# A hybrid mLSTM and attention layer on one core: the first block's sums and splits in another order, and its first loads on two queues

## The chip, the cores and the metric

The kernel runs on one core of one Trainium2 chip. The metric is the device time of one execution in microseconds (us). The engines are TensorE (PE; its weight loads are PEld), VectorE (DVE), ScalarE (ACT), GpSimd (POOL) and SyncE (SP), whose queue issues nearly all transfers. The profile is of one execution, and Lnn is line nn of the kernel.

## What is computed

One layer of a streaming encoder over 2048 prompt tokens and 8 x 16 sample tokens, width 1024, in float32:

```python
qm, km, vm, om, ip, fp, qa, ka, va = split_in(x @ w_in)
hm, C1, n1, m1 = mlstm_chunkwise(qm, km, vm, logi, logf, C0, n0, m0, mchunk)   # 4 heads of 128
ha = swa_prompt(qa, ka, va, attn_sinks)                                         # or swa_step for the samples
mix = jnp.concatenate([hm, ha], axis=-1) @ w_out
h = layer_norm(DEEPNORM_ALPHA * x + mix, ln1_g, ln1_b)
f, conv_rows = conv_ffn(h, conv_prev, w_up, w_conv, b_conv, w_down)
y = layer_norm(DEEPNORM_ALPHA * h + f, ln2_g, ln2_b)
```

The case touches only the beginning of `x @ w_in`.

## The kernel before

**Splits.** Every operand of a matmul is split into a high part, which ScalarE casts (L218 for weights, L569 for tokens: `oh`), and a low part, which VectorE subtracts (L219; L570: `ol`). A product then takes three matmuls: high by high, high by low, low by high.

**Blocks and products.** The tokens go through the input projection in blocks. Block 0 has the four token tiles 0 to 3, 128 tokens each, and the sample tile 16. For each of five groups `g` of output columns, the product of the block with the weights is formed in Strassen's manner from seven products of half-sized blocks. They are numbered 1 to 7; (b, g, s) is product s of group g in block b. The products need sums of quarters of the tokens (`x_steps`: t3, t2, t4 and t1, each a VectorE pass over 128x1024) and of quarters of the weights (`split_first`, L505 to L522). The tokens' quarters are the loads 1 to 4 (`xr1` to `xr4`; load 3 holds the second half of the columns of tokens 0 and 1, and serves product 2). Ahead of the products stand direct products of each token tile with the gate and key weights `wg` (`i_direct`, L739), in four pieces. The order of products in block 0 is: the direct ones of tokens 0 and 1 (first halves of both, then second halves), of tokens 2 and 3, (0,0,1), the direct one of the sample tile, (0,0,2), (0,1,1), (0,0,7), (0,0,6), (0,0,5), (0,0,4), (0,0,3), (0,1,7). A product's result is gathered in one of three PSUM banks; products 6, 5 and 3 share one, and 7 and 4 another, so each of them waits until ScalarE or VectorE (L779, L783) has read the bank.

**Order.** TensorE's instructions keep the order in which the program is written. The other engines' orders are made by a scheduler from the order in which the program asks for them, with `i_after` (the reading of banks) at high priority. Each engine then runs its own row strictly in turn. `next_raw` asks for a weight's load and `next_split` for its split; `advance` asks for as many of both as there are buffers. A transfer takes one of eight completion semaphores in rotation, and so is issued only when the eighth transfer before it has landed.

`x_load` loads token quarters, `x_steps` sums and splits them, `x_single` does so for the sample tile. Before the change all of block 0's steps are asked for ahead of the loop over products. `warm_up` runs nine matmuls on zeros before any data comes. `t_setup` loads small constants (`k_sink`, `kw` and others), which VectorE prepares at L956 to L966.

Of the kernel before, what the change touches and what calls it, by code (L numbers as in the profile page):

```python
# [205 lines left out]
class Prog:  # L206
# [20 lines left out]
    def run(self):  # L227
        PS = bass.MemoryType.PSUM
        nb = len(OBLOCKS)
        with ExitStack() as es:  # L230
            def enter(*a, **k):
                cm = self.pool(*a, **k)
                return cm.__enter__(), cm
            close = lambda cm: cm.__exit__(None, None, None)
            self.cp = es.enter_context(self.pool("const"))
            self.dp = es.enter_context(self.pool("dram", space=bass.MemoryType.DRAM))
            es.enter_context(self.tc.manual_schedule(engines={mybir.EngineType.PE}))
            self.setup()
            self.wp = es.enter_context(self.pool("wsb"))
            self.dps = es.enter_context(self.pool("dps", 3, PS))  # L240
            self.tp, tcm = enter("tsb", side="right")
            self.tps, tpcm = enter("tps", 5, PS)
            self.xp, xcm = enter("xsb")
            self.mp, mcm = enter("isb")
            chains = Chains(self)
            self.xs, self.gates, self.i_done = {}, {}, 0
            self.i_begin()
            self.warm_up()
            chains.weave(self.i_dense())
            close(mcm)  # L250
            wx, wxcm = enter("wx1sb")
            self.unit_more(wx)
            self.mp, mcm = enter("osb")
            self.o_setup()
            for b in range(nb - 1):
                chains.weave(self.late_done(self.o_block(b)))
            chains.until(NPT - 1)
            chains.drain()
            close(tpcm)
            close(tcm)  # L260
            self.fp, fcm = enter("fsb", side="right")
            self.fup, fpcm = enter("fup", 3, PS)
            self.f_setup()
            dense = self.o_block(nb - 1)
            first = self.f_hT(0)
            next(first)
            n = 0
            for i, _ in enumerate(dense):
                if i >= 2:
                    next(first, None)  # L270

                if i in (4, 7, 10):
                    self.f_tokens(0, *{4: (1,), 7: ("t1",), 10: ("t3", 7, "t2", 6)}[i])

                if i >= 22 and n < (2, 4, 5)[min((i - 22) // 4, 2)]:
                    self.f_next()
                    n += 1
            for _ in first:
                pass
            assert not self.norms  # L280
            close(mcm)
            close(wxcm)
            close(xcm)

            self.wx, wxcm = enter("wx2sb")
            self.f2, f2cm = enter("f2sb")
            self.f3, f3cm = enter("f3sb")
            self.f_ups(n)
            close(f3cm)
            close(f2cm)  # L290
            self.f2, f2cm = enter("d2sb")
            self.f3, f3cm = enter("d3sb")
            self.f_downs()
            for cm in (f3cm, f2cm, wxcm, fpcm, fcm):
                close(cm)
# [238 lines left out]
    def x_load(self, b, *qs):  # L534
        for q in qs:
            self.xr[b, q] = r = self.x_raw(q)
            x = self.a["xq"][b][(q - 1) // 2, (q - 1) % 2]
            n = 2 if (b, q) == (0, 1) else 1
            for i in range(n):
                k = slice(i * 4 // n, (i + 1) * 4 // n)  # L540
                self.nc.sync.dma_start(r[:, k], x[:, k])

    def x_steps(self, b, *steps):

        nc, V = self.nc, self.nc.vector
        r = lambda q: self.xr[b, q]
        for s in steps:
            if s == "t3":
                self.spare = False
                self.xt = e = self.raw_slot([P, 4, HT]) if b else [self.tp.tile([P, 4, HT], F32, name="xt", tag="qk", bufs=2), False]  # L550
                V.tensor_sub(e[0], r(4), r(2))
            elif s == "t2":

                V.tensor_add(self.xt[0], self.xt[0], r(1))
            elif s == "t4":

                V.tensor_sub(r(4), r(3), self.xt[0])
                self.xt[1] = True
            elif s == "t1":

                V.tensor_sub(r(2), r(2), r(1))
            else:
                x = self.xt[0] if s in (7, 6) else r({1: 1, 2: 3, 3: 4, "b12": 2, 5: 2, 4: 4}[s])

                self.hx[b, s] = h, l = self.x_slot(4 if s == "b12" else s)
                n = 4 if (b, s) == (0, 1) else 1
                for i in range(n):
                    k = slice(i * 4 // n, (i + 1) * 4 // n)
                    nc.scalar.copy(h[:, k], x[:, k])  # L569
                    V.tensor_sub(l[:, k], x[:, k], h[:, k].bitcast(F32))  # L570

    def x_single(self, *steps):

        nc, V = self.nc, self.nc.vector
        raw = self.single_raw
        for i in steps:
            src = raw[:, 4:] if i > 1 else raw[:, :4]
            if i == 4:
                V.tensor_sub(src, src, raw[:, :4])
            self.hs[i] = t = self.tp.tile([P, 2, 4, P], F32R, name="xs", tag="pth" if i == 4 else "sc", bufs=2)  # L580
            nc.scalar.copy(t[:, 0], src)
            V.tensor_sub(t[:, 1], src, t[:, 0].bitcast(F32))
        self.hs[5] = self.hs[1]
# [7 lines left out]
    def i_dense(self):  # L591
# [2 lines left out]
        last = NG - 1  # L594

        self.next_raw()
        self.x_load(0, 1)
        self.next_raw()
        self.x_load(0, 3)
        for _ in range(2):  # L600
            self.next_raw()
# [7 lines left out]
        self.next_split()  # L609
        self.x_steps(0, 1)  # L610
        self.next_split()
        self.x_steps(0, 2)
        for _ in range(2):
            self.next_split()
        self.x_steps(0, "b12", 3)
        self.x_single(1, 2)
        self.next_raw()
        self.advance()
        self.x_steps(0, "t3", 7, "t2", 6)
        self.x_single(4)  # L620
        self.x_steps(0, "t1", 5, "t4")
        self.sb, self.trans = {}, None

        passages = [{1: ["load"], 7: ["t3", 7], 6: ["t2", 6], 2: [1], 5: [2], 3: [3, "t4"], 4: ["b12", "t1"]},
# [3 lines left out]
        for item in self.items:  # L628
# [9 lines left out]
            if item[0] == "t":  # L638
                _, b, ti, e = item
                if ("g", e, 3) not in self.wu:  # L640
                    self.advance()
                if b not in self.gates:
                    self.gates[b] = self.tp.tile([P, 5, 8], F32, name="gates", tag="gates", bufs=2)
                if b == 0 and ti == 1:
                    for h in range(2):
                        for i in range(2):
                            yield from self.i_direct(b, i, e, self.ib[i * 2], (h,))
                    self.i_keys(b, 0, self.ib[0])
                    self.i_keys(b, 1, self.ib[2])
                    self.advance()  # L650
                    continue
                ps = self.bank([P, 512], "pg") if ti == 4 else self.ib[ti % 2 * 2]
                yield from self.i_direct(b, ti, e, ps)
                self.i_keys(b, ti, ps)
                if ti == 3 and b or ti == 4:
                    self.release(4)
                    self.x_steps(b, 4)
                    if b:
                        self.x_steps(b, 5)
                self.advance()  # L660
                continue
            _, b, g, s = item
            if item not in self.wu:
# [23 lines left out]
                self.x_pair(0, (7, 5, 2, 3).index(s))  # L687
            with self.tc.issue_after(behind) if behind and b == 0 else nullcontext():
                self.advance()

            if (b, g) in ((1, 1), (nb - 2, 1), (nb - 1, 0), (nb - 1, 2)):

                steps = (6, 5, 3)
# [1513 lines left out]
```

## Time and profile before

| | us |
|---|---|
| median of three runs | 2295.34 (2293.25 to 2296.85) |
| profiled execution, its own time | 2293.86 |
| its span in the profile | 2292.10 |
| TensorE busy | 2273.5 (99%) |
| VectorE busy | 1809.8 (79%) |
| ScalarE busy | 1272.4 (56%) |

The granted clock of TensorE is 0.999 over the span. The page's slices show TensorE at nine tenths or more nearly everywhere, so time is to be looked for in the stretches where it is not. In the rows that are ordered by time the columns are start, duration, engine, line, operation, output and input; brackets hold the idle time before the row and who ended it.

### The profile page before, as it was taken

To read this page: it belongs to the slowest core of one execution; us is meant where nothing else is said; L and a number is where in the kernel's file an instruction comes from. 1 tells how busy PE (TensorE), PEld (TensorE's weight loads), DVE (VectorE), ACT (ScalarE), POOL (GpSimd) and SP (SyncE) were. 2 spreads that over 40 slices of the span, in tenths; PEclk is the share of its full clock that TensorE was granted. 3 is DMA by queue.
4 is the path that set the end of the run, shared out by engine and by line. 5 is a ranking of instruction groups with operands and counts; after the bars stand their busy time and mean duration, and the time that the engine had idled before them with its cause. 6 is when DMAs were issued, how large, how long until landed. Compare 5 with 4: busy or idle time off the path is not lost.

```text
span 2292.1 us, 39775 instructions
## 1 busy us (share of the span) xinstructions
PE 2273.5 (99%) x14293; PEld 2090.7 (91%) x14293; DVE 1809.8 (79%) x3068; ACT 1272.4 (56%) x2373; POOL 278.7 (12%) x509
## 2 busy tenths in 40 slices
PE   8999999999999999999999999999999999999998
PEld 8999999999878778999999999999999988888876
DVE  8777687777788879998778777778766786895987
ACT  5453476776766656555556555555555644444442
POOL 0001001000121110211112000013111200200200
PEclk9999999999999999999999999999999999999999
DMA  8989998898998867898778999988998786757752
GB/s 283 323 305 322 316 315 276 273 313 297 333 317 263 278 219 262 314 328 299 282 269 271 302 303 306 312 265 288 324 290 264 255 292 216 254 169 224 252 157 85
DMA packets 302133, 631.30 MB, mean 275 GB/s; under 512 B 47404, under 2 KB 140656, under 8 KB 301936
## 3 DMA queue, kind: packets, MB, share of 16 engines
q1 hardware_dynamic: 297264, 615.06, 79.2%
q0 software_dynamic: 3520, 10.56, 1.5%
q10 hardware_dynamic: 1152, 3.15, 0.4%
q8 instruction: 113, 1.85, 0.3%
q14 instruction: 84, 0.69, 0.1%
HBM read 457.02 MB, written 171.64 MB: 274 GB/s over the span
## 4 chain that ended last, share of the span: by engine, by line
PE 83%; DVE 3%; issue 1%; ACT 1%; DMA 1%; POOL 0%; SPq 0%; DVEq 0%; ACTq 0%; POOLq 0%
PE dps L1882 20%; PE fup L1882 20%; PE dps L713 8%; PE fup L2090 7%; PE dps L2090 7%; PE fht L2090 6%; PE dps L223 3%; PE dps L225 2%; PE dps L224 2%; PE ppo L1359 1%; PE ppt L1353 1%; PE psc L1314 1%; PE fht L1706 1%; PE pcu L1231 1%; PE dps L739 1%
## 5 line engine op out<-in xcount | busy, mean ns | idle before, releaser
L1882 PE MATMUL fup<-hh,uw 128*128 128x384 f32 (+1 forms) x1848 | 478.2, 328 | 0.0
L1882 PE MATMUL dps<-hh,uw 128*128 128x384 f32 (+1 forms) x1848 | 478.0, 328 | 0.0
L1882 PEld LDWEIGHTS fup<-hh,uw 128*128 128x128 f32 x1848 | 330.2, 188 | 0.0
L1882 PEld LDWEIGHTS dps<-hh,uw 128*128 128x128 f32 x1848 | 330.1, 188 | 0.0
L1882 PE MATMUL fup<-hl,uw 128*128 128x384 f32 (+1 forms) x924 | 302.9, 328 | 1.0 <-DVE hl L219 1.0
L1882 PE MATMUL dps<-hl,uw 128*128 128x384 f32 (+1 forms) x924 | 302.7, 328 | 0.0
L1940 DVE SCALAR_TENSOR_TENSOR cc<-u,cw,cc 128x768 f32<-128x768 f32 (+1 forms) x264 | 258.0, 978 | 39.3 <-ACT cc L1938 30.8
L713 PE MATMUL dps<-w,oh 128*128 128x256 f32 x1344 | 254.8, 285 | 0.1
L218 ACT CAST uw<-wraw 128x1024 fp32r<-128x1024 f32 x126 | 123.3, 978 | 228.2 <-PE dps L2090 122.2
L219 DVE TENSOR_TENSOR w<-wraw,w 128x1024 fp32r<-128x1024 f32 (+2 forms) x163 | 186.0, 1149 | 61.6 <-ACT w L218 58.6
L218 ACT CAST w<-wraw 128x1024 fp32r<-128x1024 f32 (+2 forms) x163 | 160.2, 992 | 113.8 <-PE dps L713 53.7
L713 PEld LDWEIGHTS dps<-w,oh 128*128 128x128 f32 x1344 | 210.9, 188 | 11.2 <-issue 8.1
L219 DVE TENSOR_TENSOR uw<-wraw,uw 128x1024 fp32r<-128x1024 f32 x126 | 142.2, 1129 | 61.2 <-ACT uw L218 61.2
L713 PE MATMUL dps<-w,ol 128*128 128x256 f32 x672 | 188.2, 280 | 0.0
L1882 PEld LDWEIGHTS fup<-hl,uw 128*128 128x128 f32 x924 | 173.7, 188 | 1.7 <-DVE hl L219 1.6
L1882 PEld LDWEIGHTS dps<-hl,uw 128*128 128x128 f32 x924 | 173.7, 188 | 0.0
L2090 PE MATMUL fup<-uw,fu 128*128 128x512 f32 x726 | 173.6, 396 | 0.0
L713 PE MATMUL dps<-oh,w 128*128 128x256 f32 x896 | 168.0, 283 | 3.9 <-DVE w L219 2.2
L2090 PEld LDWEIGHTS fup<-uw,fu 128*128 128x128 f32 x726 | 136.5, 188 | 32.7
L2090 PE MATMUL dps<-uw,fu 128*128 128x512 f32 x660 | 164.8, 396 | 0.0
L2090 PEld LDWEIGHTS dps<-uw,fu 128*128 128x128 f32 x660 | 124.1, 188 | 29.8
L713 PEld LDWEIGHTS dps<-oh,w 128*128 128x128 f32 x896 | 140.0, 188 | 10.1 <-issue 4.1
(320 smaller groups left out, 4567.6 us busy)
## 6 DMA issues: line engine op xcount, KB each, us to landing
uw<-zw SPq DMA_DIRECT2D x176, 512.0 KB, 5.0
zw<-uw SPq DMA_DIRECT2D x88, 512.0 KB, 3.3
w<-zws SPq DMA_DIRECT2D x72, 512.0 KB, 6.0
wv<-wup SPq DMA_DIRECT2D x66, 512.0 KB, 5.2
wraw<-wi SPq DMA_DIRECT2D x65, 512.0 KB, 5.2
wraw<-zt SPq DMA_DIRECT2D x60, 512.0 KB, 4.3
wraw<-wdn SPq DMA_DIRECT2D x45, 512.0 KB, 4.9
wraw<-wo SPq DMA_DIRECT2D x40, 512.0 KB, 5.1
```

The source lines that it names most:

```text
L218: nc.scalar.copy(hi, src)
L219: return nc.vector.tensor_sub(lo, src, hi.bitcast(F32)).ins
L223: mm(out, ah, bh, start=start, stop=False)
L224: mm(out, ah, bl, start=False, stop=False)
L225: mm(out, al, bh, start=False, stop=stop)
L713: mm(o, l, r, start=s in (1, 7) and c == k == i == 0, stop=k == 3 and i == 2, skip_group_check=True)
L739: mm(o, x, w, start=k == i == 0, stop=k == KD - 1 and i == 2, skip_group_check=True)
L1231: nc.tensor.matmul(ps[:, i], kw[:, h], v1[:, h], start=True, stop=True)
L1314: nc.tensor.matmul(ps[kvh][:, j, :nk], q[rs, j0 + j], k[rs, sel], start=i == 0, stop=i == 2)
L1882: mm(ps, l[:, k], r[:, k], start=s in (1, 7) and k == 0 and i == 0, stop=k == 3 and i == 2, skip_group_check=True)
L1940: V.scalar_tensor_tensor(c[:, v], u[:, i:i + n], w[i], c[:, v], op0=ALU.mult, op1=ALU.add)
L2090: mm(ps, l[:, k, c], r[:, k], start=s in (1, 4, 7) and u == 0 and k == 0 and i == 0, stop=u == nu - 1 and k == n - 1 and i == 2, skip_grou ...
```

## The change

It has four parts. The first two of block 0's token loads, 1 and 3, are issued by ScalarE's queue, load 3 in two halves, and load 1 is asked for before `warm_up`. The split of load 3 is made in two halves, with a split of gate weights after each. Of the sums and splits of block 0 only t3 and 7 stay ahead of the loop; t2 and 6 follow the direct product of the sample tile, t1 and 5 follow (0,0,2), t4, 4 and the sample's step 4 follow (0,1,1). The matmuls and their order stay as they are.

```diff
@@ run
             self.i_begin()
+            self.next_raw()
+            self.x_load(0, 1)
             self.warm_up()
@@ x_load
-            n = 2 if (b, q) == (0, 1) else 1
+            first = b == 0 and q in (1, 3)
+            n = 2 if first else 1
             for i in range(n):
                 k = slice(i * 4 // n, (i + 1) * 4 // n)
-                self.nc.sync.dma_start(r[:, k], x[:, k])
+                (self.nc.scalar if first else self.nc.sync).dma_start(r[:, k], x[:, k])
@@ x_steps
-    def x_steps(self, b, *steps):
+    def x_steps(self, b, *steps, between=None):
...
-                n = 4 if (b, s) == (0, 1) else 1
+                n = 4 if (b, s) == (0, 1) else 2 if (b, s) == (0, 2) else 1
                 for i in range(n):
...
                     V.tensor_sub(l[:, k], x[:, k], h[:, k].bitcast(F32))
+                    if between:
+                        between()
@@ i_dense
-        self.next_raw()
-        self.x_load(0, 1)
         self.next_raw()
         self.x_load(0, 3)
...
         self.next_split()
-        self.x_steps(0, 2)
-        for _ in range(2):
-            self.next_split()
+        self.x_steps(0, 2, between=self.next_split)
         self.x_steps(0, "b12", 3)
         self.x_single(1, 2)
         self.next_raw()
         self.advance()
-        self.x_steps(0, "t3", 7, "t2", 6)
-        self.x_single(4)
-        self.x_steps(0, "t1", 5, "t4")
+        self.x_steps(0, "t3", 7)
...
                 if ti == 3 and b or ti == 4:
                     self.release(4)
-                    self.x_steps(b, 4)
                     if b:
-                        self.x_steps(b, 5)
+                        self.x_steps(b, 4, 5)
                 self.advance()
+                if ti == 4:
+                    self.x_steps(0, "t2", 6)
                 continue
...
                 self.advance()
+            if (b, g, s) == (0, 0, 2):
+                self.x_steps(0, "t1", 5)
+            elif (b, g, s) == (0, 1, 1):
+                self.x_steps(0, "t4", 4)
+                self.x_single(4)
```

ScalarE's first rows before. `xr_228` is load 1, `xr_233` load 3, `xr_239` load 2 and `xr_241` load 4; `wraw_226` to `wraw_237` are the four pieces of gate weights.

```order
L569 ACT_TABLE_LOAD
L569 CAST oh_254<-xr_228 128x256
L218 CAST w_251<-wraw_226 128x528
L569 CAST oh_254<-xr_228 128x256 x3
L218 CAST w_264<-wraw_231 128x528
L569 CAST oh_267<-xr_233 128x1024
L218 CAST w_271<-wraw_235 128x528
L218 CAST w_274<-wraw_237 128x528
L569 CAST oh_277<-xr_239 128x1024
L747 COPY zev_385<-dps_210 128x256
L748 COPY gates_336<-dps_210 128x8
L569 CAST oh_281<-xr_241 128x1024
```

The same place now, where load 1 is `xr_215`, load 3 `xr_233`, load 2 `xr_240` and load 4 `xr_242`:

```order
L544 DMA xr_215<-xq 128x512 x2
L544 DMA xr_233<-xq 128x512 x2
L218 ACT_TABLE_LOAD
L218 CAST w_252<-wraw_213 128x528
L572 CAST oh_255<-xr_215 128x256 x4
L218 CAST w_265<-wraw_231 128x528
L572 CAST oh_268<-xr_233 128x512
L218 CAST w_272<-wraw_236 128x528
L572 CAST oh_268<-xr_233 128x512
L218 CAST w_277<-wraw_238 128x528
L572 CAST oh_280<-xr_240 128x1024
L572 CAST oh_284<-xr_242 128x1024
```

Four transfers stand ahead of the table load, and the cast of load 4 has moved from behind the copy of token 0's result (`zev_385`) to right behind the cast of load 2.

VectorE before, from the sum t1 to the weights of (0,1,1), which are `w_508`. `xt` holds t3 and then t2; `ol_318`, `ol_332`, `ol_323` are the low parts of 7, 5 and 6.

```order
L561 TENSOR_TENSOR xr_239<-xr_239,xr_228 128x1024
L878 TENSOR_TENSOR rb_430<-zev_427,ropet_247 128x2x32
L505 TENSOR_TENSOR wraw_291<-wraw_291,wraw_292 128x1024
L570 TENSOR_TENSOR ol_318<-xt_315,oh_317 128x1024
L570 TENSOR_TENSOR ol_332<-xr_239,oh_331 128x1024
L554 TENSOR_TENSOR xt_315<-xt_315,xr_228 128x1024
L879 TENSOR_TENSOR zev_427<-zev_427,ropet_247 128x128
L557 TENSOR_TENSOR xr_241<-xr_233,xt_315 128x1024
L570 TENSOR_TENSOR ol_323<-xt_315,oh_322 128x1024
L880 TENSOR_TENSOR zev_427<-zev_427,rb_430 128x128
L219 TENSOR_TENSOR w_508<-wraw_313,w_507 128x1024
```

VectorE now, from behind the sum t3 (held in `xt_318`) to the weights of (0,1,1), now `w_496`:

```order
L884 TENSOR_TENSOR zev_373<-zev_373,ropet_246 128x128
L507 TENSOR_TENSOR wraw_294<-wraw_294,wraw_295 128x1024
L573 TENSOR_TENSOR ol_321<-xt_318,oh_320 128x1024
L885 TENSOR_TENSOR zev_373<-zev_373,rb_376 128x128
L510 TENSOR_TENSOR wraw_295<-wraw_295,wraw_296 128x1024
L882 TENSOR_TENSOR rb_385<-zev_382,ropet_246 128x2x32
L883 TENSOR_TENSOR rb_385<-zev_382,ropet_246 128x2x32
L557 TENSOR_TENSOR xt_318<-xt_318,xr_215 128x1024
L884 TENSOR_TENSOR zev_382<-zev_382,ropet_246 128x128
L564 TENSOR_TENSOR xr_240<-xr_240,xr_215 128x1024
L885 TENSOR_TENSOR zev_382<-zev_382,rb_385 128x128
L219 TENSOR_TENSOR w_496<-wraw_316,w_495 128x1024
```

The low parts of 5 and 6 and the sum t4 no longer stand ahead of the weights of (0,1,1), and a sum of weights (L510) that followed them has moved ahead.

SyncE's queue around the small constants, before: the store of token 3's keys is `zkv3`, and `kw` is the last constant.

```order
L750 DMA zkv2_105<-zev_427 128x256
L945 DMA k_mcau_682<-mcau 128x128
L945 DMA k_mswa_684<-mswa 128x384
L945 DMA k_seg_686<-seg 4x384
L945 DMA k_sink_688<-sink 128x8
L945 DMA k_sinkx_690<-sinkx 128x1
L945 DMA k_m0_692<-m0 4x8
L945 DMA k_gm_699<-gm 128x4
L750 DMA zkv3_106<-zev_460 128x256
L964 DMA kw_702<-sel 36x4
```

And now:

```order
L755 DMA zkv2_105<-zev_415 128x256
L505 DMA zws0_0_71<-wraw_294 128x1024
L763 DMA zqk0_67<-zev_592 128x2x256
L505 DMA zws0_3_74<-wraw_297 128x1024
L755 DMA zkv3_106<-zev_448 128x256
L950 DMA k_sink_691<-sink 128x8
L950 DMA k_sinkx_693<-sinkx 128x1
L950 DMA k_m0_695<-m0 4x8
L950 DMA k_gm_702<-gm 128x4
L969 DMA kw_705<-sel 36x4
```

Four constants that stood ahead of the store of token 3's keys now stand behind it, and two stores of weight sums ahead of all of them.

## The prediction

> **What bounds the kernel now.** I read the page first, then TensorE's waits, then the busy time by stretch, then the time-ordered rows of TensorE, VectorE, ScalarE and the sync queue for the first 60 us, because the change moves instructions only there. The page's busy line:
>
> ```profile
> PE 2273.5 (99%) x14293; PEld 2090.7 (91%) x14293; DVE 1809.8 (79%) x3068; ACT 1272.4 (56%) x2373; POOL 278.7 (12%) x509
> ```
>
> TensorE is idle for 18.6 of 2292.1 us. A change that leaves its matmuls alone can win only part of that. Its waits in the first 100 us (who waits, for whom: total, times, longest):
>
> ```profile
> PE dps L713 <- DVE w L219: 2.2, 2, 1.4
> PE dps L328 <- DVE zero L323: 2.0, 1, 2.0
> PE dps L739 <- DVE w L219: 1.0, 1, 1.0
> PE dps L713 <- ACT zev L779: 0.7, 1, 0.7
> ```
>
> The 2.0 is the start. The rest lies at four places (start, duration, engine, and in brackets the idle time before):
>
> ```profile
> 11.40 0.39 PE L739 MATMUL dps<-w,oh 128*128 128x264 f32 x1 [0.96 <-DVE w L219]
> ...
> 33.24 0.50 PE L713 MATMUL dps<-oh,w 128*128 128x256 f32 x2 [1.39 <-DVE w L219]
> 41.40 0.51 PE L713 MATMUL dps<-oh,w 128*128 128x256 f32 x2 [0.80 <-DVE w L219]
> 44.86 0.39 PE L713 MATMUL dps<-oh,w 128*128 128x256 f32 x1 [0.69 <-ACT zev L779]
> ...
> 49.32 0.39 PE L713 MATMUL dps<-oh,w 128*128 128x256 f32 x1
> ```
>
> By the order of products these begin the second half of tokens 0 and 1 (11.40), product (0,1,1) (33.24), (0,0,6) (41.40), (0,0,5) (44.86) and (0,0,4) (49.32). The last follows VectorE's read of the same PSUM bank, in the second fence below. Busy time by stretch (length; busy of PE, PEld, DVE, ACT, POOL; clock; share of the DMA engines; GB/s):
>
> ```profile
> 2.00:6.30 4.30, 4.30 (x11) 3.15 (x11) 1.98 (x8) 1.88 (x6) 0.00 (x0) 1.00 0.85 278
> 6.30:20.00 13.70, 12.74 (x95) 12.28 (x95) 10.69 (x22) 9.24 (x21) 0.00 (x0) 1.00 1.00 398
> ...
> 14.46:49.26 34.80, 31.92 (x265) 31.18 (x263) 34.69 (x59) 18.42 (x31) 0.00 (x0) 1.00 0.76 269
> ...
> 57.40:250.00 192.60, 192.60 (x1670) 188.57 (x1670) 146.31 (x232) 88.37 (x137) 10.81 (x9) 1.00 0.91 319
> 250.00:340.00 90.00, 87.02 (x776) 82.24 (x775) 61.35 (x132) 55.99 (x127) 7.65 (x13) 1.00 0.94 314
> ```
>
> The third row decides the case: between 14.46 and 49.26 VectorE works 34.69 of 34.80 us. TensorE's waits there are the shape of one queue that is full, seen from the outside. VectorE's rows at both ends and in the middle:
>
> ```profile
> 14.46 1.23 DVE L570 TENSOR_TENSOR ol<-xr,oh 128x1024 fp32r<-128x1024 f32 x1 [1.16 <-ACT oh L569]
> ...
> 25.89 1.22 DVE L570 TENSOR_TENSOR ol<-xt,oh 128x1024 fp32r<-128x1024 f32 x1
> 27.02 1.22 DVE L570 TENSOR_TENSOR ol<-xr,oh 128x1024 fp32r<-128x1024 f32 x1
> ...
> 43.54 0.14 DVE L956 TENSOR_SCALAR nsinkx<-k_sinkx 128x1 f32<-128x1 f32 x1
> ...
> 48.57 0.69 DVE L783 SCALAR_TENSOR_TENSOR zev<-dps,zev 128x512 f32<-128x512 f32 x1
> ```
>
> One 128x1024 pass costs 27.02 − 25.89 = 1.13 us from start to start. From 57.40 to 250 TensorE has no gap at all, so what it wins in front it keeps that far.
>
> **The change part by part.**
>
> *Order of the passes.* Before, seven passes on the first block's tokens (t3, t1, low parts 7 and 5, t2, t4, low part 6) stand ahead of the weights for (0,1,1), and an eighth (low part 4) ahead of those for (0,0,7) and (0,0,6). Now each stands where its product comes. Nothing of size is added: one more split of a 128x1024 pass into two of 512, three more instructions. Gain on TensorE's side: the waits at 33.24 and 41.40, 1.39 + 0.80 us. The 0.69 at 44.86 is (0,0,5) waiting for the bank that (0,0,6) leaves; the two still follow each other, so it stays.
>
> *Early weights and tokens.* The 0.96 at 11.40 comes from ScalarE's and VectorE's order. ScalarE's rows:
>
> ```profile
> 0.74 1.28 ACT L569 ACT_TABLE_LOAD   x1 [0.74 <-PEq L2199]
> 4.21 0.40 ACT L569 CAST oh<-xr 128x256 fp32r<-128x256 f32 x1 [2.19 <-DMA xr<-xq]
> 4.84 0.63 ACT L218 CAST w<-wraw 128x528 fp32r<-128x528 f32 x1 [0.23 <-DMA wraw<-wg]
> 5.38 1.01 ACT L569 CAST oh<-xr 128x256 fp32r<-128x256 f32 x3
> 6.30 0.63 ACT L218 CAST w<-wraw 128x528 fp32r<-128x528 f32 x1
> 8.42 1.05 ACT L569 CAST oh<-xr 128x1024 fp32r<-128x1024 f32 x1 [1.49 <-DMA xr<-xq]
> ...
> 11.00 1.05 ACT L569 CAST oh<-xr 128x1024 fp32r<-128x1024 f32 x1 [0.46 <-DMA xr<-xq]
> 13.04 0.37 ACT L747 COPY zev<-dps 128x256 f32<-128x256 f32 x1 [0.99 <-PE dps L739]
> ...
> 13.37 1.07 ACT L569 CAST oh<-xr 128x1024 fp32r<-128x1024 f32 x1
> ```
>
> and the sync queue's:
>
> ```profile
> 0.74 0.39 SPq L541 DMA_DIRECT2D xr<-xq  x1
> 1.19 0.42 SPq L458 DMA_DIRECT2D wraw<-wg  x1
> ...
> 2.60 0.43 SPq L541 DMA_DIRECT2D xr<-xq  x1
> ...
> 4.03 1.02 SPq L541 DMA_DIRECT2D xr<-xq  x2
> ...
> 9.11 3.50 SPq L589 DMA_DIRECT2D wraw<-wi  x4
> ```
>
> ScalarE stood 1.49 us until 8.42 for the third token load (issued 2.60, 5.8 us earlier). With two queues that load's halves are issued at about 1.66 and 2.12 and land by 7.5 to 7.9. Casting from 4.4 (the first gate weights landed at 4.84 and are now issued at 0.74, not 1.19; 0.54 for a gate weight, 0.31 a quarter, some 0.53 a half token tile, from the rows above and half of 1.05), ScalarE is through all four gate weights at 4.4 + 4 × 0.54 + 4 × 0.31 + 2 × 0.53 = 8.9, VectorE behind it at about 10; TensorE reaches the second half at 11.40 − 0.96 = 10.4. So the 0.96 goes. ScalarE's four issues cost its queue 4 × 0.46 = 1.8 us (spacing of the sync queue's) ahead of the 1.28 table load: ready at 3.9, under the 4.21 at which data first came. That cover is thin, and its other price is a rival.
>
> TensorE alone would then gain 0.96 + 1.39 + 0.80 = 3.15 us by (0,0,4).
>
> *What is late next.* (0,0,4) also needs VectorE's pass of row 48.57, which stands behind the same work as before, all of it. It can come earlier only by as much as the full stretch starts earlier. That stretch starts at 14.46 with the low part of token load 4, whose cast ScalarE made only at 13.37, behind a copy that waited for TensorE until 13.04. Now that cast stands right behind the one of load 2. With load 2 landing at 11.00 as before: casts at 11.0 and 12.0, low part at 13.2: 1.2 us earlier. If the DMA engines, 0.85 busy at 278 GB/s until 6.30, ran there at the later 398, they would be 4.3 × (398 − 278) / 398 = 1.3 us ahead: load 2 lands at 9.7, and the low part of load 4 starts at 11.9, 2.5 us earlier. Behind it VectorE then wants the first product's weights at about 14.4. Their load, at 9.11 behind a wait for the third token load, now goes at about 8.3 and takes 4.0 to 7.0:
>
> ```profile
> DMA to landing us min/median/max: 4.0/6.0/7.0
> ```
>
> so 14.3 plus a 0.33 cast: 0.25 us lost. Sum: 2.5 − 0.25 = 2.25, call it 2.2, from bounds of 1.2 and 2.9 (the weights landing at once and nothing lost elsewhere). TensorE's 3.15 is larger, so VectorE's 2.2 sets (0,0,4), and a new wait of about 1 us appears before it. Between these, the weights and low parts of the reordered products are ready some 4 us ahead: counting 1.13 us a pass and 0.2 for each small one from the weights of (0,0,2) at 16.9, (0,1,1)'s are done after 8 passes at about 27, TensorE wants them at 33.24 − 1.39 − 0.96 = 30.9; the low part of (0,0,6) after 13 at about 34, wanted at 38.2.
>
> *After it* the order on every engine is the same row for row (the sync queue's from about 85 us), so all shifts by 2.2. The profiled execution took 2293.86 us (span 2292.10), 1.48 under the median of the runs shown, 2295.34; a shift carries over: 2291.7 for a like execution, **2293.1** for the median.
>
> **Rivals.**
>
> *The queues only share.* [...] In rows: the share is already 1.00 from 6.30 on, load 2 now sits behind a wait for the first token load's landing (about 4.2, against its issue at 4.03), and so it lands at 11.00 as before. Then only the cast's new place is left: 1.2 us, 2294.1. The 0.85 share before 6.30 speaks against it. [...]
>
> *VectorE does not hold.* If its stretch started early enough, all 3.15 us come: 2292.2. The 34.69 of 34.80 speaks against it.
>
> *ScalarE starts late.* Its own issues elsewhere in this trace (min/median/max ns):
>
> ```profile
> L1724 ACTq DMA_DIRECT2D hst<-zh x4: 326/340/1187, 852.0 to 866.0; - x4
> ```
>
> At 1.19 us each the table load ends at 0.74 + 4.76 + 1.28 = 6.8, casting starts 2.4 us later, load 4's is at 12.4 its low part 0.9 us earlier than before at best, and TensorE loses 2.4 of its 3.15: 0.7 is won, 2294.6. The median of 0.34 speaks against it. [...]
>
> *Given back later.* From 250 to 340 TensorE idles 3.0 us. If a transfer sets those waits (share 0.94), the 2.2 end there: 2295.3. Against it: the longest wait there is on POOL, and the rest on engines too:
>
> ```profile
> PE ppt L1526 <- POOL v L1104: 1.4, 1, 1.4
> ```
>
> *Slower: small constants.* The loads of k_sink to kw now stand on the sync queue behind the store of token 3's keys, which waits for VectorE. That store follows a VectorE row I count at about 34.1; five issues at 0.46 later kw is out at about 36.5. VectorE wants it at 43.54 − 2.25 = 41.3, ahead of row 48.57. The issue before, and landing times (last number):
>
> ```profile
> 36.91 0.40 SPq L964 DMA_DIRECT2D kw<-sel  x1
> ...
> k_sink<-sink SPq DMA_DIRECT2D x1, 4.0 KB, 3.7
> ...
> ropet<-rope SPq DMA_DIRECT2D x2, 96.0 KB, 7.7
> ```
>
> At k_sink's 3.7 it costs nothing. Above 4.8 VectorE stalls; above 7.0 the 2.2 is gone; at the rope tables' 7.7 the stall is 2.9 and the kernel 0.7 slower: 2296.0. The constants' own 3.7 speaks against it.
>
> **How the numbers follow.** Forecast 2.2 (1.7 to 2.9): 0.45. Queues share: 0.18. VectorE does not hold: 0.12. Given back: 0.10. ScalarE late: 0.08. Slower: 0.07. The runs before lie from 2293.25 to 2296.85, 2.1 below to 1.5 above their median, so a median after carries some 1.5 us of its own. The range holds 3.15 + 1.5 of gain at one end, 2290.6, and at the other the slower case, or the no-gain one with half of the spread, 2296.0. Over 0.2% (4.6 us, about what a measurement of this kernel can tell from no change) none of the cases goes by itself. The spread takes a quarter of the forecast, two fifths of the full gain and a tenth of the shared case below 2290.7: 0.18, rounded to 0.20 for later waits that may shrink too. Above 2299.9 only the slower case with more stalls behind it: 0.06. Within: 0.74.
>
> **What would show it.** Right: no TensorE wait at the starts of the second token half, (0,1,1) and (0,0,6); the low part of load 4 at 11.9 to 13.2; a TensorE wait of about 1 us for VectorE at (0,0,4), which starts at about 47.1; VectorE without a gap up to there. Wrong: the ScalarE table load ending after 4.4, a VectorE gap before nsinkx, or (0,0,4) starting before 46.3 or after 48.2. If (0,0,4) is at 47.1 and the span is not some 2.2 shorter, the loss lies between 250 and 340.

## The result, and the profile after

The changed kernel takes 2291.59 us, the median of 22 runs (2290.62 to 2293.58), against 2293.93 of the kernel before in 22 runs beside them: a ratio of 0.9988, with a 95% interval of 0.9983 to 0.9994. Timed once more among the experiments (e11) it had 2291.84 against 2294.18, ratio 0.9989 (0.9980 to 0.9998). The forecast was 2293.1 with a range of 2290.6 to 2296.0, made against the median of 2295.34 then shown: a gain of 2.2 us was forecast and 2.3 measured, with an interval of 1.4 to 3.9. (In absolute terms the forecast is 1.5 too high, since the three runs that it starts from had a median 1.4 above that of the 22.)

The profiled execution took 2291.51 us with a span of 2289.7, 2.4 less than before. The page's busy line, then TensorE's waits in the first 100 us, without the 2.0 of the start:

```profile
PE 2272.4 (99%) x14293; PEld 2088.7 (91%) x14293; DVE 1809.2 (79%) x3069; ACT 1273.2 (56%) x2374; POOL 273.1 (12%) x509
```

```profile
PE dps L744 <- ACT gates L753: 0.8, 1, 0.8
PE dps L718 <- ACT zev L784: 0.7, 1, 0.7
PE dps L744 <- DVE w L219: 0.4, 1, 0.4
PE dps L744 <- ACT w L218: 0.3, 1, 0.3
PE dps L718 <- ACT zev L776: 0.3, 1, 0.3
PE dps L718 <- DVE zev L788: 0.2, 1, 0.2
```

The lines have moved: L713 is now L718, L739 L744, L570 L573, L779 L784, L783 L788. The waits of 1.39, 0.80 and 0.96 are gone, the 0.69 stayed. In their place stand five shorter ones, of which four were not in the forecast. TensorE's rows in order of time (start, duration; idle before in brackets):

```profile
14.43 0.51 PE L744 MATMUL dps<-w,oh 128*128 128x264 f32 x2 [0.75 <-ACT gates L753]
...
23.20 1.59 PE L728 MATMUL psx<-w,xs 128*128 128x256 f32 x12
...
32.14 0.38 PE L718 MATMUL dps<-oh,w 128*128 128x256 f32 x1 [0.30 <-ACT zev L776]
...
42.81 0.39 PE L718 MATMUL dps<-oh,w 128*128 128x256 f32 x1 [0.69 <-ACT zev L784]
...
47.43 0.38 PE L718 MATMUL dps<-oh,w 128*128 128x256 f32 x1 [0.17 <-DVE zev L788]
```

They begin token 2, the sample tile's part of (0,0,1), (0,1,1), (0,0,5) and (0,0,4). Two of them have to be compared with rows of before that were not shown yet, the sample part of (0,0,1) and the start of (0,1,1); the third row is the sample part of (0,1,1):

```profile
22.97 1.59 PE L723 MATMUL psx<-w,xs 128*128 128x256 f32 x12
...
31.45 0.28 PE L713 MATMUL dps<-oh,w 128*128 128x256 f32 x1
...
35.93 1.59 PE L723 MATMUL psx<-w,xs 128*128 128x256 f32 x12
```

Before, (0,1,1) began at 31.45 and waited only ahead of its third matmul, 33.24. Now it begins 0.69 later (32.14), but then runs through, and its sample part, now at 34.97, is 0.96 earlier. (0,0,5) is 2.05 earlier (44.86 to 42.81) and (0,0,4) 1.89 (49.32 to 47.43). The sample part of (0,0,1) is not earlier at all: over the first 23 us, where the 0.96 went, TensorE lost 0.23. VectorE's rows at the two ends of its full stretch, and the stretch between:

```profile
11.51 2.44 DVE L573 TENSOR_TENSOR ol<-xr,oh 128x1024 fp32r<-128x1024 f32 x2 [0.21 <-ACT oh L572]
...
46.69 0.69 DVE L788 SCALAR_TENSOR_TENSOR zev<-dps,zev 128x512 f32<-128x512 f32 x1
```

```profile
12.60:47.00 34.40, 32.66 (x273) 32.05 (x272) 34.25 (x59) 19.11 (x34) 0.00 (x0) 1.00 0.83 292
```

The second of the two passes at 11.51 is the low part of load 4; it starts at about 12.65 (half of the 2.4 us later), before at 14.46. From there to VectorE's read of the bank that (0,0,4) waits for are 34.04 us, before 34.11. VectorE is as full as it was (34.25 of 34.40) and starts 1.8 earlier. ScalarE's first rows, where that start comes from:

```profile
0.74 1.86 ACTq L544 DMA_DIRECT2D xr<-xq  x4
2.63 1.28 ACT L218 ACT_TABLE_LOAD   x1 [2.63 <-issue]
4.54 0.63 ACT L218 CAST w<-wraw 128x528 fp32r<-128x528 f32 x1 [0.63 <-DMA wraw<-wg]
...
8.11 0.62 ACT L572 CAST oh<-xr 128x512 fp32r<-128x512 f32 x1 [0.81 <-DMA xr<-xq]
...
10.42 1.05 ACT L572 CAST oh<-xr 128x1024 fp32r<-128x1024 f32 x1
11.63 1.06 ACT L572 CAST oh<-xr 128x1024 fp32r<-128x1024 f32 x1 [0.16 <-DMA xr<-xq]
12.90 1.14 ACT L586 CAST xs<-xsr 128x512 fp32r<-128x512 f32 x2 [0.21 <-DMA xsr<-xs]
13.94 0.37 ACT L752 COPY zev<-dps 128x256 f32<-128x256 f32 x1
```

The casts of loads 2 and 4 stand at 10.42 and 11.63 (before 11.00 and 13.37). The last row is token 0's copy. It now stands behind load 4's cast and the sample tile's two casts, and token 2 needs its bank: that is the wait of 0.75.

### The profile page after: what moved, and what is told of

Read it like the earlier page. It is cut to its first block, busy times and chain, and to the rows that moved or that the text cites. A ratio compares the mean times of both kernels' runs of the same rounds, so it can differ in the third digit from the quotient of the medians.

```text
span 2289.7 us, 39785 instructions
## 1 busy us (share of the span) xinstructions
PE 2272.4 (99%) x14293; PEld 2088.7 (91%) x14293; DVE 1809.2 (79%) x3069; ACT 1273.2 (56%) x2374; POOL 273.1 (12%) x509
## 4 chain that ended last, share of the span: by engine, by line
PE 82%; DVE 4%; DMA 1%; issue 1%; ACT 1%; POOL 0%; DVEq 0%; ACTq 0%; POOLq 0%; SPq 0%
PE dps L1887 20%; PE fup L1887 20%; PE dps L718 8%; PE fup L2095 7%; PE dps L2095 7%; PE fht L2095 6%; PE dps L223 2%; PE dps L224 2%; PE dps L225 2%; PE ppo L1364 1%; PE ppt L1358 1%; PE psc L1319 1%; PE dps L744 1%; DVE w L219 1%; PE fht L1711 1%
## 5 line engine op out<-in xcount | busy, mean ns | idle before, releaser
L718 PE MATMUL dps<-w,oh 128*128 128x256 f32 x1344 | 254.8, 284 | 0.0
L718 PEld LDWEIGHTS dps<-w,oh 128*128 128x128 f32 x1344 | 210.8, 188 | 11.0 <-issue 8.1
L718 PE MATMUL dps<-w,ol 128*128 128x256 f32 x672 | 188.0, 280 | 0.0
L718 PE MATMUL dps<-oh,w 128*128 128x256 f32 x896 | 167.3, 282 | 2.0 <-ACT mr L1169 0.9
L718 PEld LDWEIGHTS dps<-oh,w 128*128 128x128 f32 x896 | 139.7, 188 | 7.9 <-issue 4.1
```

What stands on the lines that cost most here:

```text
L718: mm(o, l, r, start=s in (1, 7) and c == k == i == 0, stop=k == 3 and i == 2, skip_group_check=True)
```

## The experiments

Theory A: VectorE's row sets (0,0,4), by when its full stretch starts and how long it is; what TensorE wins ahead of that, it waits off again. Theory B: TensorE's waits add up, and each one removed is won. Since one comparison of 11 runs leaves an interval of some ±0.0009 (2 us), the traces decide, and the medians are looked at together. (0,0,4) and VectorE's read of its bank are in us from the span's start, and TensorE's wait is the one ahead of (0,0,4); the last column is a kernel's median less that of the kernel before beside it.

| | load 4's low part | VectorE's read | length | TensorE's wait | (0,0,4) | less before | median less before |
|---|---|---|---|---|---|---|---|
| before | 14.46 | 48.57 | 34.11 | 0 | 49.32 | | |
| changed | 12.65 | 46.69 | 34.04 | 0.17 | 47.43 | −1.89 | −2.34 |
| e1 order only | 15.56 | 48.39 | 32.83 | 0.78 | 49.13 | −0.19 | −0.78 |
| e5 the same again | 14.84 | 47.68 | 32.84 | 0.85 | 48.41 | −0.91 | −1.34 |
| e2 loads only | 12.52 | 48.06 | 35.54 | 0.64 | 48.79 | −0.53 | −0.81 |
| e3 one queue | 13.79 | 46.63 | 32.84 | 0.87 | 47.36 | −1.96 | −1.96 |
| e4 two sums less | 12.80 | 48.05 | | 0.64 | 48.79 | −0.53 | −0.88 |
| e6 copy first | 12.62 | 46.70 | 34.08 | 0 | 47.44 | −1.88 | −2.22 |
| e7 one queue, sums on GpSimd | 13.82 | 51.49 | | 1.19 | 52.23 | +2.91 | +3.00 |
| e8 copy first, sums on GpSimd | 12.66 | 56.40 | | 0 | 57.14 | +7.82 | +8.07 |
| e9 one queue, VectorE relieved | 14.09 | 46.13 | | 0 | 46.87 | −2.45 | +2.21 |
| e10 copy first, VectorE relieved | 12.38 | 46.46 | | 0 | 47.20 | −2.12 | −1.27 |

(Where the two low parts of loads 2 and 4 share a row, the second is taken 1.14 after its start.) But for e9 and e10 the last two columns agree within 0.6 us: what (0,0,4) wins or loses reaches the end of the kernel. That rests on the row of them together, e7 and e8 above all. A single median is not that exact: the ratios given below, from the same runs, differ from the last column by up to 0.6 us, and a single trace can differ too, as e1 and e5 show, which are one kernel.

**e1 and e5: the new order alone.** The kernel before with the changed places of the sums and splits; all loads as before.

```diff
-        self.x_steps(0, "t3", 7, "t2", 6)
-        self.x_single(4)
-        self.x_steps(0, "t1", 5, "t4")
+        self.x_steps(0, "t3", 7)
...
+                if ti == 4:
+                    self.x_steps(0, "t2", 6)
...
+            if (b, g, s) == (0, 0, 2):
+                self.x_steps(0, "t1", 5)
+            elif (b, g, s) == (0, 1, 1):
+                self.x_steps(0, "t4", 4)
+                self.x_single(4)
```

> The kernel before with the changed order of sums and splits alone; loads, queues and the split of load 3 stay as before. Theory A (VectorE's full stretch sets product (0,0,4), and its start is not moved): the waits at (0,1,1) and (0,0,6), 1.39 and 0.80, vanish and come back as one wait of about 2.2 before (0,0,4), which starts at 49.1 to 49.5 as before (49.32); ratio 1.0000 to 1.0002, about 2294. Theory B (TensorE's waits add up): both waits vanish for good, (0,0,4) at about 47.1, ratio 0.9990, about 2291.7.

> The same kernel as e1 once more, for a trace whose first 20 us run at full clock (in e1's the clock was 0.54 to 0.61 from 8 to 12 us and the first product began 1.09 later than before). If VectorE sets (0,0,4) by start plus length of its stretch: load 4's low part at 14.3 to 14.6 as before, then 32.8 as in e1 (one weight sum fewer ahead), so VectorE's pass at 47.1 to 47.4 and (0,0,4) at 47.9 to 48.2. If TensorE's waits add up: (0,0,4) at 47.0 to 47.2. If the order does nothing: 49.1 to 49.5.

The ratios are 0.9996 (0.9987 to 1.0005) and 0.9994 (0.9985 to 1.0002). In e1's trace TensorE's clock was 0.57 from 8 to 12 us, hence e5. VectorE's rows of e5 at the two ends, and TensorE's (0,0,4):

```profile
14.84 1.23 DVE L570 TENSOR_TENSOR ol<-xr,oh 128x1024 fp32r<-128x1024 f32 x1 [1.16 <-ACT oh L569]
...
47.68 0.67 DVE L787 SCALAR_TENSOR_TENSOR zev<-dps,zev 128x512 f32<-128x512 f32 x1
```

```profile
48.41 0.38 PE L717 MATMUL dps<-oh,w 128*128 128x256 f32 x1 [0.85 <-DVE zev L787]
```

In e1 (0,0,4) stands where A has it, 49.13, but behind a first product that came late, and with a wait of 0.78, not 2.2; in e5 none of the three numbers came. In e5 the wait at (0,1,1) vanishes, that at (0,0,6) shrinks from 0.80 to 0.41, and 0.85 comes back at (0,0,4), as A has it; but (0,0,4) is 0.9 earlier, which A as I stated it (no gain) did not allow. The reason is in VectorE's row. The stretch is 32.84 instead of 34.11, because the scheduler puts one sum of the next group's weights, 1.13 us, and one small pass behind the read of the bank instead of ahead of it. Two traces with starts 0.72 apart have the same length to 0.01 and end 0.71 apart: start plus length holds.

**e2: the new loads alone.** The changed kernel with the edit of e1 undone.

> The changed kernel with the old order of sums and splits: only the queues of loads 1 and 3, the early load 1 and the split of load 3 in two remain. Theory A: VectorE's stretch starts at about 12.6 and is as long as before, so (0,0,4) is at 47.3 to 47.7 with TensorE waits of about 1 to 1.5 us in all still at (0,1,1) and (0,0,6); ratio 0.9988 to 0.9992, about 2291.6. Theory B: of the three waits only the 0.96 goes, and of that the new wait of token 2 (0.75) takes most back: (0,0,4) at 48.4 to 49.1, ratio 0.9996 to 0.9999.

(0,0,4) is at 48.79, ratio 0.9995 (0.9986 to 1.0004), between the two. VectorE starts at 12.5 as A says, but is stopped once on the way, until a store of a weight sum has read the buffer that it overwrites next:

```profile
36.21 1.23 DVE L512 TENSOR_TENSOR wraw<-wraw 128x1024 f32<-128x1024 f32 x1 [1.27 <-DMA zws<-wraw]
```

and TensorE waits at (0,0,6) as before, for weights that come too late in the row, and then for the read of the bank; at (0,1,1) there is no wait:

```profile
40.23 0.51 PE L714 MATMUL dps<-oh,w 128*128 128x256 f32 x2 [1.16 <-DVE w L219]
...
48.79 0.38 PE L714 MATMUL dps<-oh,w 128*128 128x256 f32 x1 [0.64 <-DVE zev L784]
```

So in these traces the halves give 0.91 and 0.53, together 1.89: an early start is worth little with the old order, and the new order little without the early start.

**e3: one queue.**

```diff
-                (self.nc.scalar if first else self.nc.sync).dma_start(r[:, k], x[:, k])
+                self.nc.sync.dma_start(r[:, k], x[:, k])
```

> The changed kernel with loads 1 and 3 issued by SyncE again (load 1 still early, both in halves). If only the order of splits and casts matters and two queues share what one would give: load 2 lands within 0.4 of the changed kernel (its cast at 10.4), (0,0,4) at 47.2 to 47.8, ratio 0.9988. If the second queue itself brings the loads forward: four more issues of 0.45 stand ahead of loads 2 and 4, load 2's cast is at 11.4 to 12.2, load 4's low part at 13.7 to 14.4, (0,0,4) at 48.3 to 49.2, ratio 0.9993 to 1.0000.

Ratio 0.9994 (0.9985 to 1.0003). Each side is right on one number, (0,0,4) for sharing and load 4's low part for the second queue. Load 2 is cast at 11.00, as late as before, so the second queue did bring it forward, by 0.58. But (0,0,4) is where the changed kernel has it:

```profile
11.00 1.05 ACT L572 CAST oh<-xr 128x1024 fp32r<-128x1024 f32 x1 [0.61 <-DMA xr<-xq]
12.37 0.37 ACT L752 COPY zev<-dps 128x256 f32<-128x256 f32 x1 [0.32 <-PE dps L744]
```

```profile
46.63 0.68 DVE L788 SCALAR_TENSOR_TENSOR zev<-dps,zev 128x512 f32<-128x512 f32 x1
```

```profile
47.36 0.39 PE L718 MATMUL dps<-oh,w 128*128 128x256 f32 x1 [0.87 <-DVE zev L788]
```

Token 0's copy stands here ahead of load 4's cast, as before the change, so there is no wait at token 2; VectorE starts 1.14 later than in the changed kernel, and its row is 1.20 shorter, as in e5. TensorE is 0.87 ahead of VectorE: the wait of about 1 us that I forecast for the changed kernel is seen here. So the same place of (0,0,4) is reached another way, and that the two agree is chance. (The execution traced is the slowest of e3's eleven, 2294.16: TensorE idles 2.71 us from 340 to 1000, before 0.68. The gain shows in the median, not in this one.)

**e4: two sums less.** The changed kernel leaves out the sums t1 and t4 of block 0, so that products 5 and 4 are formed from unsummed tokens.

```diff
-                V.tensor_sub(r(4), r(3), self.xt[0])
+                if b:
+                    V.tensor_sub(r(4), r(3), self.xt[0])
...
-                V.tensor_sub(r(2), r(2), r(1))
+                if b:
+                    V.tensor_sub(r(2), r(2), r(1))
```

> The changed kernel without the sums t1 and t4 of block 0, two VectorE passes of 1.13 us (products 5 and 4 are then formed from unsummed tokens). As predicted (VectorE sets (0,0,4) by about 1 us): (0,0,4) at 46.3 to 46.6, ratio 0.9983 to 0.9985. By the trace after (the wait there is only 0.17, and TensorE's own chain is next): (0,0,4) at 47.1 to 47.3, VectorE's pass of the bank some 2 us ahead of need, ratio 0.9987 to 0.9988. If VectorE alone sets the pace all along: (0,0,4) at 45.2, ratio 0.9979.

None of the three came: 48.79, ratio 0.9998 (0.9989 to 1.0007). The scheduler filled the place with other work. On ScalarE a weight's cast, which waits for TensorE to free its buffer, now stands ahead of the read that (0,0,5) waits for, and on VectorE the gates' chain stands ahead of the read for (0,0,4):

```profile
42.10 1.04 ACT L218 CAST w<-wraw 128x1024 fp32r<-128x1024 f32 x1 [1.66 <-PE dps L720]
43.05 0.59 ACT L786 ACTIVATE zev<-dps 128x512 f32<-128x512 f32 x1
```

```profile
43.70 0.38 PE L720 MATMUL dps<-oh,w 128*128 128x256 f32 x1 [1.56 <-ACT zev L786]
```

It says nothing between A and B: leaving work out also moved work.

**e6: token 0's copy first.** The sample tile's casts are asked for behind the copy.

```diff
-        self.x_single(1, 2)
...
-        nc.scalar.copy(self.gates[b][:, ti, :], ps[:, :8])
+        gate = nc.scalar.copy(self.gates[b][:, ti, :], ps[:, :8])
+        if b == ti == 0:
+            with self.tc.issue_after(gate.ins):
+                self.x_single(1, 2)
```

> The changed kernel with the sample tile's two casts asked for behind token 0's copy on ScalarE. The wait of 0.75 at token 2 goes or falls below 0.3. If VectorE sets (0,0,4): VectorE's row is as long as after, its pass at 46.5 to 46.9, (0,0,4) at 47.3 to 47.6 with a wait of 0.7 to 0.9 (after: 0.17), and the time is as after, ratio to before 0.9988. If TensorE's waits add up: (0,0,4) at 46.7 to 46.9, ratio 0.9985.

The wait at token 2 is gone, and the sample part of (0,0,1) comes at 22.30, 0.90 earlier. Nothing of it is left at (0,0,4), 47.44; the ratio is 0.9990 (0.9982 to 0.9999). The wait is not where I expected it, though: it is already at (0,1,1),

```profile
32.10 0.39 PE L717 MATMUL dps<-oh,w 128*128 128x256 f32 x1 [1.13 <-ACT zev L778]
```

which needs the bank that ScalarE reads behind a cast that waits for VectorE's sum:

```profile
30.51 1.05 ACT L218 CAST w<-wraw 128x1024 fp32r<-128x1024 f32 x1 [2.41 <-DVE wraw L512]
31.47 0.58 ACT L778 COPY zev<-dps 128x512 f32<-128x512 f32 x1
```

This is the cleanest sign that B is wrong. TensorE was given 0.9 us and lost it to VectorE, by way of ScalarE's row. But the row of VectorE's that counted here is the sum that this cast waits for (29.26), not the read of the bank; e10 will show the same. The changed kernel has its 0.30 at the same place and time (32.14), for the same reason.

**e7 and e8: two sums on GpSimd.** To shorten VectorE's row, t1 and t4 of block 0 go to GpSimd, which is idle there; e7 from e3, e8 from e6.

```diff
-                V.tensor_sub(r(4), r(3), self.xt[0])
+                (V if b else nc.gpsimd).tensor_sub(r(4), r(3), self.xt[0])
...
-                V.tensor_sub(r(2), r(2), r(1))
+                (V if b else nc.gpsimd).tensor_sub(r(2), r(2), r(1))
```

> e3 (one queue) with the sums t1 and t4 of block 0 on GpSimd; by the order of VectorE's row two sums leave it and one weight sum and one small pass come in, some 1.0 us less ahead of its pass of the bank. If VectorE sets (0,0,4): e3's wait of 0.87 there shrinks to 0.0 to 0.3 and (0,0,4) comes at 46.5 to 46.8, since TensorE's own chain from (0,0,5) takes 4.46 at least; ratio 0.9983 to 0.9986. If VectorE is not what is waited for: (0,0,4) at 47.3 as in e3, ratio 0.9988. If GpSimd's passes are late or slow VectorE down: a wait before (0,0,5) or (0,0,4), 47.5 or later.

> e6 with the sums t1 and t4 on GpSimd. VectorE's row is one pass shorter than in e6. If VectorE sets (0,0,4) there: 46.4 to 46.7, ratio 0.9983 to 0.9986. ScalarE's row has one step of the gates' chain between its two reads of the shared bank; if that stands for VectorE, (0,0,4) is at 47.4 or later, as in e4.

Ratios 1.0013 (1.0005 to 1.0022) and 1.0033 (1.0021 to 1.0045): both slower. e7's rows of GpSimd and VectorE:

```profile
22.92 2.41 POOL L564 TENSOR_TENSOR xr<-xr 128x1024 f32<-128x1024 f32 x1 [22.08 <-DVE xt L554]
37.39 6.65 POOL L560 TENSOR_TENSOR xr<-xr,xt 128x1024 f32<-128x1024 f32 x1 [12.05 <-DMA zws<-wraw]
```

```profile
22.98 3.43 DVE L507 TENSOR_TENSOR wraw<-wraw 128x1024 f32<-128x1024 f32 x1
...
45.14 1.22 DVE L573 TENSOR_TENSOR ol<-xr,oh 128x1024 fp32r<-128x1024 f32 x1 [3.35 <-ACT oh L572]
```

A VectorE pass of 1.22 takes 3.43 beside GpSimd's first, which is 2.41 long, and ends 1.08 after it. GpSimd's second starts while VectorE's passes follow each other without a gap, takes 6.65, and ends 2.2 after VectorE's last of them (41.8). The cast, the low part and (0,0,5) waited for it.

**e9 and e10: VectorE relieved another way.** The weights of (0,1,7) and the gates' chain are asked for only behind VectorE's read of the bank; e9 from e3, e10 from e6.

```diff
+        if u == ("p", 0, 1, 7) and not self.read5:
+            return False
...
-            self.chains.hold = item[0] == "t" and item[1] > 0
+            self.chains.hold = item[0] == "t" and item[1] > 0 or not self.read5
...
-            add(u4)
+            read = add(u4)
...
+            if (b, g) == (0, 0):
+                self.read5 = read
+                return read
...
+        with self.tc.issue_after(self.read5) if b == 0 else nullcontext():
+            return self.gate_logs_of(b)
```

> e3 (one queue) with VectorE relieved without GpSimd: the weights of product (0,1,7) and the gates' chain are asked for only behind VectorE's read of the bank that (0,0,4) needs; two 128x1024 passes (2.27 us) leave the row ahead of it. If VectorE sets (0,0,4) in e3: the wait of 0.87 there falls to 0.1 or less, VectorE's pass at 45.9 to 46.1 directly behind ScalarE's copy, (0,0,4) at 46.4 to 46.6 (e3: 47.36; before: 49.32), ratio 0.9983 to 0.9987. If VectorE is not what is waited for: 47.3, and e3's ratio.

> e6 with the same relief of VectorE ahead of (0,0,4). In e6 TensorE did not wait there, it had lost 1.13 at (0,1,1) and 0.69 at (0,0,5). If only the place where TensorE waits counts: (0,0,4) stays at 47.3 to 47.6 and the time is e6's, ratio 0.9988 to 0.9991, though VectorE is through some 2 us sooner. If VectorE's total ahead of (0,0,4) counts wherever it lies: 46.3 to 46.6, ratio 0.9984.

In e9 VectorE waits for ScalarE's copy instead of the other way round, and (0,0,4) follows (0,0,5) without a wait:

```profile
46.13 0.69 DVE L790 SCALAR_TENSOR_TENSOR zev<-dps,zev 128x512 f32<-128x512 f32 x1 [1.39 <-ACT zev L786]
```

e3's 0.87 is gone, as A says; (0,0,4) is at 46.87 rather than 46.5 because all of TensorE ran 0.3 to 0.4 later from the start. e10 goes against A as I stated it:

```profile
31.86 0.39 PE L719 MATMUL dps<-oh,w 128*128 128x256 f32 x1 [1.13 <-ACT zev L780]
...
47.20 0.39 PE L719 MATMUL dps<-oh,w 128*128 128x256 f32 x1
```

```profile
46.46 0.69 DVE L792 SCALAR_TENSOR_TENSOR zev<-dps,zev 128x512 f32<-128x512 f32 x1 [3.49 <-ACT zev L788]
```

VectorE's row is much shorter and VectorE is idle for 3.49 us before its read, yet (0,0,4) is only 0.24 earlier than in e6, and by 0.24 everything in e10 is earlier, from load 4's low part on. From (0,1,1) to (0,0,4) TensorE takes 15.34 us in both. So in e6 VectorE's row sets (0,0,4) only up to the weight sum that (0,1,1) waits for by way of ScalarE; from there it is TensorE's own chain, with the 0.69 at (0,0,5). In the changed kernel the two are level: 15.29 with a wait of 0.17 for VectorE, and in e11 15.33 without one.

Both e9 and e10 pay later for what was put off, at (0,1,6), which needs a copy that ScalarE now makes behind late casts: 1.00 in e10 (ratio 0.9996, 0.9987 to 1.0005) and 2.78 in e9 (1.0010, 1.0001 to 1.0019), where more was lost behind it. e9's TensorE row, and busy time by stretch around it (length; PE, PEld, DVE, ACT, POOL; clock; DMA share; GB/s):

```profile
60.15 0.39 PE L720 MATMUL dps<-oh,w 128*128 128x256 f32 x1 [2.78 <-ACT dps L817]
```

```profile
60.00:62.00 2.00, 1.85 (x11) 1.85 (x12) 2.00 (x3) 1.07 (x2) 0.00 (x0) 0.73 1.12 264
62.00:64.00 2.00, 2.00 (x12) 2.00 (x11) 1.93 (x3) 0.00 (x0) 0.00 (x0) 0.50 0.86 320
64.00:66.00 2.00, 2.00 (x17) 2.00 (x17) 1.41 (x2) 1.30 (x2) 0.00 (x0) 0.92 1.00 401
```

The granted clock was 0.73, 0.50 and 0.92 in the three stretches of 2 us behind the gap. As an estimate, what they lack to full clock is 2 × (0.27 + 0.50 + 0.08) = 1.7 us more. −2.45 + 2.78 + 1.7 = 2.0, near the 2.21 measured.

**e11: the changed kernel again.**

> The changed kernel itself, timed beside e9 and e10. (0,0,4) at 47.2 to 47.6 with a wait of 0.1 to 0.3; ratio 0.9987 to 0.9991; token 2's wait of 0.7 to 0.8 and a shorter one at (0,1,1) are there again.

(0,0,4) at 47.47, without a wait, so the forecast of 0.1 to 0.3 there did not come; token 2's wait is 0.53, not 0.7 to 0.8, and (0,1,1)'s 0.29. The ratio is given at the top.

No version beats the changed kernel by what can be measured: e6 and e3 have medians of 2291.63 and 2291.96.

## Why the prediction was right, and where it was not

**The bound: right in kind, but only just there.** VectorE's full row sets TensorE's pace, and the gain is the earlier start of that row. Forecast 2.2 by (0,0,4), measured 1.89, within the bounds of 1.2 and 2.9. e3 and e5 show it at the place forecast: TensorE waits 0.87 and 0.85 for VectorE's read, and start plus length gives that read. In the changed kernel VectorE's read and TensorE come to (0,0,4) within 0.2 us of each other; e6 and e10 show that TensorE is held there from an earlier row of VectorE's, the weight sum ahead of (0,1,1). Both follow the start of the stretch, which is why the forecast held.

**The start of the row: right in kind, 0.7 too early.** Load 4's low part was to start at 11.9 and did at 12.65. The step that failed is the landing of load 2, put at 9.7 by letting the DMA engines run at 398 GB/s before 6.30. The last of its completions in the trace is at 10.40. The engines ran at 331 (278 before):

```profile
2.00:6.30 4.30, 4.25 (x11) 3.02 (x11) 1.86 (x8) 2.78 (x5) 0.00 (x0) 1.00 0.96 331
```

By the working's own formula that is 4.3 × (331 − 278) / 398 = 0.57 us, and load 2's cast did come 0.58 earlier than in e3. A second step failed at the same place: ScalarE was to be through the gate weights at 8.9 and was at 10.4 (9.76 + 0.63), so the cast could not have begun at 9.7 in any case. And the sum had no term for load 4's own landing, which cost the 0.16 before its cast at 11.63. The other term, load 4's cast directly behind load 2's, was right and the larger one. The 0.25 to be lost at the first product's weights was not lost: their load was issued at 9.23, not 8.3 (SyncE's queue waited for the second half of load 3, which had the same completion semaphore and landed at 9.21), but VectorE was late as well, its only gap before them is 0.15, and the stretch is 0.07 shorter than before.

**TensorE's own gain of 3.15: wrong.** It was to be more than VectorE's by about 1, so that a wait of 1 us would stand before (0,0,4); there it is 0.17, or none in e11. The step that failed is "so the 0.96 goes", as if nothing came in its place. TensorE did run into the second half of tokens 0 and 1 without a wait, but ScalarE was late from its start: the first cast waited for data until 4.54, and load 3's first half was cast at 8.11, not 7.5 to 7.9. So TensorE waits already in the first half, 0.30 for the cast of the second piece of weights and 0.36 for its low part. And I named who had stood ahead of load 4's cast, but not who now stands behind it: token 0's copy, 0.75. With the 0.30 at (0,1,1) these are 1.71 in place of 0.96. e6 shows that the 0.75 cost nothing in the end, since VectorE takes back, at (0,1,1), what TensorE wins there. The error was hidden by the bound, and by luck: TensorE came to (0,0,4) 0.17 ahead of VectorE in one trace of the changed kernel and not at all in the other. Two readings were off besides: the rows at 11.40, 33.24 and 41.40 do not begin what I said they begin. They are a second matmul and twice a third one, which need the low part of the weights; the waits are the same.

**The passes between: right on VectorE, incomplete on ScalarE.** (0,1,1)'s weights were counted done at about 27 and were at 27.8:

```profile
26.56 1.22 DVE L219 TENSOR_TENSOR w<-wraw,w 128x1024 fp32r<-128x1024 f32 x1
```

The bank that (0,1,1) overwrites was not looked at; ScalarE reads it behind a cast that waits for VectorE.

**The rivals.** "The queues only share" gave load 2 at 11.00 with a gain of 1.2: a part of it holds. With one queue (e3) the gain at (0,0,4) is 1.96, much the same, so what the second queue brings forward, 0.58 of load 2, is not needed; but e3 has a row in another order, so this does not show that the second queue by itself is worth nothing. The share in 2.00 to 6.30 rose from 0.85 to 0.96 with two queues and is 0.97 in e3 with one; but the engines moved 331 GB/s with two queues and 265 in e3. "ScalarE starts late": the table load ended at 3.91, as counted, and the first cast began at 4.54, after 0.63 us for data. "Given back later" did not happen: from 57.40 to 340 TensorE idles 2.65 us, before 2.98. "Slower": the small constant kw was issued at 36.95 (forecast 36.5) and VectorE reached the first of them at 41.68 without a gap.

**The size of the median.** 1.89 lies at (0,0,4). The rest of the 2.34 lies in no one place: 0.33 of TensorE's idle time is gone from 57.40 to 340. What else there is of it is below what the runs can tell, and that the median's gain meets the forecast to 0.1 is luck: the term behind the forecast was 0.3 too large.

## What to carry to other kernels

When one engine's row is full from end to end, count when it starts and how much stands ahead of the row that is waited for; the waits seen on other engines say where it is felt, not what removing them is worth. It can be felt first at an earlier row than the last, and by way of a third engine: taking work out behind that row then wins nothing (e10). When an instruction is moved up a strict queue, name the one that it now stands in front of and who waits for that one. Taking work away from such a row, or putting it off, makes a scheduler fill the place: read the new order on every engine, up to where the work put off is wanted.

## What the runs showed of the hardware

The long passes of e7 and e8, and those beside them, are float32 passes with two inputs over 128x1024. A VectorE pass begun 0.06 us behind a GpSimd pass took 3.43 in e7 and ended 1.08 after that one; the same line's next pass, with GpSimd idle, took 1.22 (47.49). GpSimd passes that started amid VectorE's back-to-back passes took 6.65 (e7) and 9.10 (e8) instead of 2.41, and both ended 2.2 us after the last of these VectorE passes. e8's other GpSimd pass, begun 0.02 us behind a VectorE pass, took 3.46, and the VectorE pass behind that one 3.42. What decides how long each takes is not shown.

TensorE's granted clock behind e9's wait of 2.78 was 0.73, 0.50 and 0.92 in stretches of 2 us, as the rows above have it. In e7 TensorE waited 0.42 before 38.39 and 1.94 before 40.71; the clock was 0.90 from 40 to 42 us, then 0.50,

```profile
42.00:44.00 2.00, 2.00 (x12) 2.00 (x11) 0.00 (x0) 0.00 (x0) 2.00 (x1) 0.50 0.60 163
```

and 0.75 from 44 to 46. By the estimate of 1.7 us more, e9's wait of 2.78 cost about 4.5 in all; the same sum for e7 is 2 × (0.10 + 0.50 + 0.25) = 1.7, of which a part fell on the wait of 1.40 that came next anyway. Behind the gaps of 1.39 (before, 33.24) and 1.56 (e4, 43.70) the clock was 1.00. The length of a gap alone does not tell these traces apart: behind a gap of 1.08 before 8.32, with one of 0.36 before 6.37, e1's clock was 0.61 from 8 to 10 us and 0.54 from 10 to 12, and behind one of 1.08 before 7.80 e3's was 1.00. What decides it is not shown.
